# Two decoder layers on one core: the order of three engines between the halves of the layers, written by hand without weight splits

## The chip, the cores and the metric

The kernel runs on one core of a Trainium2 chip. A core has five engines that work beside each other, each taking its own instructions in order and waiting for the others through semaphores: TensorE (PE in the rows, its weight loads PEld), VectorE (DVE), ScalarE (ACT), GpSimd (POOL) and SyncE (SP), which here starts all the transfers. The metric is the device time of one execution in microseconds (us). TensorE's granted clock is at full speed throughout the profiled execution.

## The reference

`x` is 256 rows of 1024 numbers in float32. Layer 0 normalises it, projects it, runs two kinds of attention and an output projection, adds the result to `x`, and then a feed-forward. Layer 1 has a gated spatial mixer and a convolution in place of the attention. Cut to its frame:

```python
for i in range(DEPTH):                     # two layers
    h = rms_norm(x, attn_norm_g[i])
    if i % 2 == 0:
        mix = even_mixer(h, ...)           # differential and block-sparse attention, 8 heads each
    else:
        mix = odd_mixer(h, ...)            # spatial gating, 31-tap causal convolution
    x = x + mix
    x = x + swiglu(rms_norm(x, ffn_norm_g[i]), ffn_w_in[i], ffn_w_out[i])

def rms_norm(x, g):
    return x * rsqrt(mean(x * x, axis=-1) + EPS) * g

def swiglu(h, w_in, w_out):
    g, u = split(h @ w_in, 2)              # 1024 -> 2 x 2816
    return (silu(g) * u) @ w_out
```

## The kernel before, in words

**Precision by splits.** Each float32 operand of a product is kept as two parts: `hi` (rounded by ScalarE while it copies) and `lo` (VectorE subtracts `hi` from the value). A product is three matmuls, hi x hi, hi x lo and lo x hi (`passes`, L225 to L227). Weights come in blocks of 1 MB by SyncE into three buffers `raw`, and each block is split in two halves: `whi` (L131, ScalarE) and `wlo` (L135, VectorE, for some blocks GpSimd). `pump(n)` writes out the next n of these waiting split steps; `ahead` puts a block's four steps in the waiting list; `held` keeps the list from being worked off beside the matmuls.

**The order.** TensorE's order is the program's. The other engines' order is made by a list scheduler, except inside `in_order(...)`, where the named engines keep the order in which the code writes their instructions. Instructions from outside such a region can still be placed between those of the region.

**The boundary, `close`.** It stands three times between a projection and what follows: site 0 between the attention's output projection and the first feed-forward, site 1 between that feed-forward and the odd mixer, site 2 between the odd mixer's output projection and the second feed-forward. The 256 rows are two halves m = 0, 1 of 128, the 1024 columns two halves n. While TensorE still does the last eight steps (`tail_steps`) for m = 1, half m = 0 is closed: VectorE adds the residual into `xs` (L358), ScalarE squares it with a row sum `ss` (L302), VectorE makes `st` (L307, L308), GpSimd raises it to the power -0.5 (`rm`, L310), VectorE multiplies the rows with it (`scr`, L331, one for each n). Then `norm_T` (L340) transposes one column half on TensorE, and `split` copies it to `xT` as hi (ScalarE, L239) and lo (VectorE, L240). Half m = 1 follows the same way inside `follow`, beside the first steps of the next part (`first_steps` of the feed-forward: 16 steps of three matmuls of 256 columns for m = 0, or `gv_steps(0)`: 8 steps of 512 columns). `first_steps` takes columns 0 to 511 in its first four steps and the others after them. `first_T` (L444) transposes the first feed-forward result; it comes six steps into `first_steps` for m = 1 and needs the silu (ScalarE, L436) and a product (VectorE, L437) of the 16 steps for m = 0.

The tables that place these pieces, at the head of the kernel: `SPLITS[site]` how many split steps are written out in the region, `N_T0` and `N_T1` after which step the transposes stand.

**The start and the odd mixer.** `prep` makes the products of a query or key projection that need no scale, and a `scaled` step (L627) for keys; `qk_T` (L638) transposes the result. `PUMPS` says how many split steps stand between. In the odd mixer `spatial` (L1127 to L1135) is TensorE's gating product, ScalarE's scaling L1131, GpSimd's sum and product, ScalarE's hi and GpSimd's lo; L1156 is a one-column silu that loads ScalarE's table ahead of its use.

Of the kernel before, what the change touches and what calls it, by code (L numbers as in the profile page):

```python
# [22 lines left out]
F32 = mybir.dt.float32  # L23
FR = mybir.dt.float32r
AF = mybir.ActivationFunctionType
# [3 lines left out]
P = 128  # L29
S = 256  # L30
# [13 lines left out]
PACE = (3, 1, 2, 1)  # L44

WARM = (5, 4)
PUMPS = (0, 9, 7)

SCALE_FROM, T_FROM = 1, 2
SCALE_AT = 4  # L50
T_AT = 3


LAG = 2
# [1 line left out]
SHARES = (5, 4, 4, 5, 4, 1, 7, 5, 1, 1, 5, 4, 0, 1, 5, 0, 3, 2, 2, 7, 2)  # L56


SPLITS = ((2, 3, 7), (12, 4, 0), (7, 3, 5))
N_T0 = (5, 4, 5)  # L60
N_T1 = (10, 5, 10)


TAP_RATE = 0.55
# [6 lines left out]
def trunk_kernel(ctx: ExitStack, tc: tile.TileContext, a: dict, out: bass.AP):  # L71
    nc = tc.nc
# [5 lines left out]
    small = ctx.enter_context(tc.tile_pool(name="small", bufs=3))  # L78
# [15 lines left out]
    plan, blocks, todo = [], {}, deque()  # L94
# [76 lines left out]
    def pump(n):  # L171
        for _ in range(min(n, len(todo))):
            b, f, step = todo.popleft()
            step(f)
            if step == b.split_lo:
                b.left[f] = 0
                if f == 1:
                    b.load_next()
# [36 lines left out]
    for j in range(2):  # L215
        plan_w(("gu", j), a["odd_w_in"][0], 0, KT, j * 256, 256, "c", lo_engine=nc.gpsimd)
    plan_out("oo", a["odd_w_out"][0], KT, lo_engine=nc.gpsimd)
    for b in (blocks["cg", 0], blocks["ca", 0]):
        b.lo_engine[1] = nc.vector
    blocks["oo", 4].lo_engine = [nc.vector] * 2  # L220
    plan_ffn(1)

# [19 lines left out]
    def in_order(*engines):  # L242

        region = ExitStack()
        region.enter_context(tc.manual_schedule(engines={getattr(mybir.EngineType, e) for e in engines}))
        return region
# [5 lines left out]
    ident = consts.tile([P, P], F32, name="ident")  # L252
# [26 lines left out]
    def col(name, i):  # L279
        return vec[:, rows[name] + i:rows[name] + i + 1]  # L280
# [40 lines left out]
        nc.sync.dma_start(g, bcast(src))  # L321
        return g

    def norm_rows(m, ss, gB, splits):

        r = row_factor(ss)
        pump(splits)
        xn = []
        for n in range(2):
            xn.append(scratch())  # L330
            nc.vector.scalar_tensor_tensor(xn[n], xs[:, m, n * 512:(n + 1) * 512], r, gB[:, n * 512:(n + 1) * 512],  # L331
                                           op0=ALU.mult, op1=ALU.mult)
        return xn

    def norm_T(m, n, xn, xT, ptag):

        pt = ptag()
        ms = slice(m * P, (m + 1) * P)
        for j in range(4):
            nc.tensor.transpose(pt[:, j * P:(j + 1) * P], xn[n][:, j * P:(j + 1) * P], ident)  # L340
        split(xT[0][:, 4 * n:4 * n + 4, ms], xT[1][:, 4 * n:4 * n + 4, ms], pt.rearrange("p (a b) -> p a b", b=P))
# [30 lines left out]
    def close(site, lhs, ws, k0, pss, gB, ptag, tail0=True):  # L372


        xT = new_xT()
        ss = [small.tile([P, 2], F32, name="ss") for _ in range(MT)]

        def end(m, n):
            residual(m, n, pss)
            square(m, n, ss[m])  # L380

        if tail0:
            for n, k in tail_steps(lhs, ws, k0, 0, pss, BY_COLS):
                if (n, k) == (0, 3):
                    end(0, 0)
        else:
            end(0, 0)
        held[0] = True
        region = in_order("DVE", "Pool")
        end(0, 1)  # L390
        xn0 = norm_rows(0, ss[0], gB, SPLITS[site][0])
        for i, (n, k) in enumerate(tail_steps(lhs, ws, k0, 1, pss, BY_BLOCK)):
            if i == 3 and ws[0].index + 4 < len(plan):
                plan[ws[0].index + 4].ahead()
            if i == N_T0[site]:
                norm_T(0, 0, xn0, xT, ptag)
                pump(SPLITS[site][1])
            if k == 3:
                end(1, n)
        norm_T(0, 1, xn0, xT, ptag)  # L400
        xn1 = norm_rows(1, ss[1], gB, SPLITS[site][2])

        def follow(steps, ptag):

            for i, _ in enumerate(steps):
                if 0 <= i - N_T1[site] < 2:
                    norm_T(1, i - N_T1[site], xn1, xT, ptag)
            held[0] = False
            region.close()

        return xT, follow
# [74 lines left out]
    xT = new_xT()  # L486
    rx = []
    with tc.tile_pool(name="attn", bufs=1) as ap, tc.tile_pool(name="pat", bufs=1, space=bass.MemoryType.PSUM) as pat:
# [165 lines left out]
        def prep(name, ps, m, n, want_scaled):  # L654
            t1, scaled = qk_prep(name, ps, m, n, want_scaled)
            pending.append((name, t1, m))
            to_scale.append(scaled)
# [3 lines left out]
        pump(PUMPS[0])  # L661
        prep("dk", ps_dk[0], 0, 32, True)
        pump(PUMPS[1])
        prep("dk", ps_dk[1], 1, 32, True)
        pump(PUMPS[2])
        held[0] = False
        start.close()

# [172 lines left out]
        def projections(jobs):  # L841


            for name in jobs:
                ws = [blocks[name, h] for h in range(2)]
                for m in range(MT):
                    turn = turns[0]
                    turns[0] += 1
                    for k, ps in enumerate(project(ws, m)):
                        if k == SCALE_AT and turn >= SCALE_FROM and to_scale:  # L850
                            to_scale.popleft()()
                        if k == T_AT and turn >= T_FROM and pending:
                            qk_T(*pending.popleft())
                        if ps is None:
                            yield
                    if name in ("dv", "mv"):
                        v_prep(name, ps, m)
                    else:
                        prep(name, ps, m, 32 if name[0] == "d" else 64, name[1] == "k")
                    yield  # L860
# [140 lines left out]
    with tc.tile_pool(name="odd", bufs=1) as op, tc.tile_pool(name="pod", bufs=1, space=bass.MemoryType.PSUM) as pod:  # L1001
# [120 lines left out]
        def spatial(p):  # L1122
            pg = mm_bank() if p % 2 else tq()
            for c in range(MT):
                for h in range(2):
                    g = 2 * p + h
                    nc.tensor.matmul(pg[h * 64:(h + 1) * 64, c * P:(c + 1) * P], gn[:, c, g * 64:(g + 1) * 64],  # L1127
                                     wsT[:, g, :], start=True, stop=True)
            sgt = scratch()[:, :S]
            sgv = sgt.rearrange("p (a b) -> p a b", b=P)  # L1130
            nc.scalar.activation(sgt, pg[:, :S], AF.Copy, scale=col("ln_g", p))  # L1131
            nc.gpsimd.tensor_tensor(sgv, sgv, biasT[:, p, None, :].to_broadcast([P, MT, P]), op=ALU.add)
            nc.gpsimd.tensor_tensor(sgt, sgt, guT[:, p, :], op=ALU.mult)
            nc.scalar.activation(cT[0][:, p, :], sgt, AF.Copy)
            nc.gpsimd.tensor_tensor(cT[1][:, p, :], sgt, cT[0][:, p, :].bitcast(F32), op=ALU.subtract)  # L1135

        pool_order = in_order("Pool")
        gated(0)
# [11 lines left out]
            next(taps)  # L1150
        for m in range(MT):
            gv_norm(m)
        last = project_gu(1)
        with tc.issue_after(last.ins):

            nc.scalar.activation(small.tile([P, 2], F32, name="st2")[:, 0:1], ident[:, 0:1], AF.Silu)  # L1156
        for p in range(4):
            spatial(p)
            for _ in range(2):
                next(taps)  # L1160
        run(taps)
# [167 lines left out]
```

## Time and profile before

| | |
|---|---|
| Median of three runs | 614.56 us (613.72 to 616.35) |
| The profiled execution's own time | 616.31 us |
| Its span, first to last instruction | 614.6 us |
| Busy: TensorE, VectorE, ScalarE, GpSimd | 600.3, 409.7, 345.9, 96.7 us |
| TensorE's weight loads | 512.3 us, beside the matmuls |

Busy time is the time in which an engine has an instruction running. TensorE's matmuls overlap each other in the profile, so its busy time also holds small delays between starts. The profiled execution is 0.3% above the median; differences are worked out in its times and then put onto the median.

### The profile page before, as it was taken

To read this page: it belongs to the slowest core of one execution; us is meant where nothing else is said; L and a number is where in the kernel's file an instruction comes from. 1 tells how busy PE (TensorE), PEld (TensorE's weight loads), DVE (VectorE), ACT (ScalarE), POOL (GpSimd) and SP (SyncE) were. 2 spreads that over 40 slices of the span, in tenths; PEclk is the share of its full clock that TensorE was granted. 3 is DMA by queue.
4 is the path that set the end of the run, shared out by engine and by line. 5 is a ranking of instruction groups with operands and counts; after the bars stand their busy time and mean duration, and the time that the engine had idled before them with its cause. 6 is when DMAs were issued, how large, how long until landed. Compare 5 with 4: busy or idle time off the path is not lost. (4 is left out here: it accounts for less than half of the span.)

```text
span 614.6 us, 8908 instructions
## 1 busy us (share of the span) xinstructions
PE 600.3 (98%) x3420; PEld 512.3 (83%) x3420; DVE 409.7 (67%) x716; ACT 345.9 (56%) x623; POOL 96.7 (16%) x89
## 2 busy tenths in 40 slices
PE   7989999999999999999999999999999999999997
PEld 5867777788888888888886999878988888888886
DVE  3799998648666648664447499877667666664421
ACT  5766768646555596653346955475555556554310
POOL 1951221001000000000004495541000000000000
PEclk9999999999999999999999999999999999999999
DMA  7947216226766527555563463145665556455301
GB/s 243 328 174 272 71 67 206 69 69 207 258 209 185 189 91 274 206 182 176 193 203 102 139 232 130 51 151 182 218 204 185 167 197 206 166 179 204 138 0 69
DMA packets 72791, 104.32 MB, mean 170 GB/s; under 512 B 3068, under 2 KB 56492, under 8 KB 72748
## 3 DMA queue, kind: packets, MB, share of 16 engines
q1 hardware_dynamic: 72748, 103.74, 50.5%
q8 instruction: 27, 0.44, 0.3%
q14 instruction: 16, 0.13, 0.1%
HBM read 102.69 MB, written 1.05 MB: 169 GB/s over the span
## 5 line engine op out<-in xcount | busy, mean ns | idle before, releaser
L131 ACT ACTIVATE whi<-raw 128x1024 fp32r<-128x1024 f32 (+1 forms) x192 | 197.6, 1041 | 175.4 <-PE mm L233 79.4
L135 DVE TENSOR_TENSOR wlo<-raw,whi 128x1024 fp32r<-128x1024 f32 (+1 forms) x174 | 210.1, 1213 | 123.4 <-ACT whi L131 121.8
L233 PE MATMUL mm<-xT,whi 128*128 128x512 f32 x640 | 226.0, 398 | 0.0
L234 PE MATMUL mm<-xT,wlo 128*128 128x256 f32 x640 | 179.6, 281 | 0.0
L233 PEld LDWEIGHTS mm<-xT,whi 128*128 128x128 f32 x640 | 120.1, 188 | 28.9 <-issue 0.2
L234 PEld LDWEIGHTS mm<-xT,wlo 128*128 128x128 f32 x640 | 120.9, 189 | 0.0
L227 PE MATMUL mm<-whi,hT_lo 128*128 128x512 f32 (+1 forms) x176 | 66.5, 378 | 0.0
L226 PE MATMUL mm<-wlo,hT_hi 128*128 128x512 f32 (+1 forms) x176 | 66.5, 378 | 0.0
L225 PE MATMUL mm<-whi,xT 128*128 128x512 f32 (+1 forms) x176 | 66.0, 375 | 0.4 <-ACT xT L545 0.4
L225 PE MATMUL mm<-whi,hT_hi 128*128 128x512 f32 (+1 forms) x176 | 66.4, 377 | 0.0
L227 PE MATMUL mm<-whi,xT 128*128 128x512 f32 (+1 forms) x176 | 63.0, 358 | 1.2 <-DVE xT L240 1.1
L226 PE MATMUL mm<-wlo,xT 128*128 128x512 f32 (+1 forms) x176 | 62.6, 355 | 0.0
L135 POOL TENSOR_TENSOR wlo<-raw,whi 128x1024 fp32r<-128x1024 f32 (+1 forms) x18 | 41.3, 2331 | 21.9 <-ACT whi L131 21.9
L227 PEld LDWEIGHTS mm<-whi,xT 128*128 128x128 f32 x176 | 33.6, 191 | 7.1 <-DVE xT L240 2.0
L225 PEld LDWEIGHTS mm<-whi,xT 128*128 128x128 f32 x176 | 33.6, 191 | 6.9 <-issue 1.3
L225 PEld LDWEIGHTS mm<-whi,hT_hi 128*128 128x128 f32 x176 | 33.1, 188 | 6.4
L226 PEld LDWEIGHTS mm<-wlo,hT_hi 128*128 128x128 f32 x176 | 33.1, 188 | 6.4
L227 PEld LDWEIGHTS mm<-whi,hT_lo 128*128 128x128 f32 x176 | 33.1, 188 | 6.3
L310 POOL TENSOR_TENSOR rm<-st,neg_half 128x1 f32<-128x1 f32 x8 | 8.0, 1002 | 186.1 <-DVE st L308 186.1
L464 DVE TENSOR_TENSOR scr<-mm,scr 128x256 f32<-128x256 f32 x80 | 33.2, 417 | 5.7 <-ACT scr L463 5.7
L226 PEld LDWEIGHTS mm<-wlo,xT 128*128 128x128 f32 x176 | 33.7, 192 | 3.8 <-DVE wlo L135 0.2
L1077 DVE SCALAR_TENSOR_TENSOR cv<-cpad,cw,cv 128x256 f32<-128x256 f32 x87 | 35.8, 479 | 0.3
(226 smaller groups left out, 843.3 us busy)
## 6 DMA issues: line engine op xcount, KB each, us to landing
raw<-in_ffn_w_in SPq DMA_DIRECT2D x44, 1024.0 KB
raw<-in_ffn_w_out SPq DMA_DIRECT2D x22, 1024.0 KB
raw<-in_even_w_in SPq DMA_DIRECT2D x10, 1024.0 KB
raw<-in_odd_w_in SPq DMA_DIRECT2D x8, 1024.0 KB
raw<-in_even_w_out SPq DMA_DIRECT2D x4, 1024.0 KB
raw<-in_odd_w_out SPq DMA_DIRECT2D x4, 1024.0 KB
xs<-in_x SPq DMA_DIRECT2D x4, 256.0 KB
raw<-in_even_w_in SPq DMA_DIRECT2D x4, 256.0 KB
```

What stands on the lines that cost most here:

```text
L131: nc.scalar.activation(self.half(f)[0][:, r], self.source(f)[:, r], AF.Copy)
L135: self.lo_engine[f].tensor_tensor(lo[:, r], self.source(f)[:, r], hi[:, r].bitcast(F32), op=ALU.subtract)
L225: nc.tensor.matmul(ps, lhs[0], rhs[0], start=first, stop=False)
L226: nc.tensor.matmul(ps, lhs[0], rhs[1], start=False, stop=False)
L227: nc.tensor.matmul(ps, lhs[1], rhs[0], start=False, stop=last)
L233: nc.tensor.matmul(bank, w[0], x[2][:, k, :, :].rearrange("p a b -> p (a b)"), start=k == 0, stop=False)
L234: nc.tensor.matmul(bank[:, :S], w[1], x[0][:, k, :], start=False, stop=k == KT - 1)
L310: nc.gpsimd.tensor_tensor(r, t[:, 1:2], neg_half[:, :1], op=ALU.pow)
L464: nc.vector.tensor_tensor(s, bank[:, :S], s, op=ALU.add)
L1077: nc.vector.scalar_tensor_tensor(conv[:, ct, :] if t == TAPS - 1 else acc, cpad[:, ct, t:t + S], cw[:, t, ct:ct + 1], acc, op0=ALU.mult, o ...
```

## The change

At the three sites the region now holds ScalarE's order too, and all waiting split steps are written out ahead of it (`pump(len(todo))`). Inside, `SPLITS` is now two numbers per site, (0, 0), (2, 2) and (0, 0): ahead of and behind the second half's normalisation. The transposes of m = 0 stand behind steps 5 and 6 everywhere; those of m = 1 behind steps 12 and 15 of `first_steps` at sites 0 and 2 (10 and 11 before), and behind 6 and 7 of `gv_steps` at site 1 (5 and 6 before). At the start the scaling of the first `dk` half is written out between the splits, and the transposes of the second one stand behind step 7 of their projection. The silu that loads a table moves behind the second `spatial` scaling. One block's low half goes from GpSimd to VectorE. No arithmetic changes.

```diff
-PUMPS = (0, 9, 7)
-SCALE_FROM, T_FROM = 1, 2
+PUMPS = (0, 5, 4, 7)
+SCALE_FROM, T_FROM = 2, 2
-T_AT = 3
+T_AT = (3, 3, 3, 7, 3, 3, 3, 3, 3, 3, 3, 3)
-SPLITS = ((2, 3, 7), (12, 4, 0), (7, 3, 5))
-N_T0 = (5, 4, 5)
-N_T1 = (10, 5, 10)
+SPLITS = ((0, 0), (2, 2), (0, 0))
+N_T0 = (5, 6)
+N_T1 = ((12, 15), (6, 7), (12, 15))
...
-    for b in (blocks["cg", 0], blocks["ca", 0]):
-        b.lo_engine[1] = nc.vector
+    blocks["cg", 0].lo_engine[1] = nc.vector
+    blocks["ca", 0].lo_engine = [nc.vector] * 2
...
-    def norm_rows(m, ss, gB, splits):
+    def norm_rows(m, ss, gB):
         r = row_factor(ss)
-        pump(splits)
...
         held[0] = True
-        region = in_order("DVE", "Pool")
+        pump(len(todo))
+        region = in_order("DVE", "Pool", "Activation")
         end(0, 1)
-        xn0 = norm_rows(0, ss[0], gB, SPLITS[site][0])
+        xn0 = norm_rows(0, ss[0], gB)
         for i, (n, k) in enumerate(tail_steps(lhs, ws, k0, 1, pss, BY_BLOCK)):
             if i == 3 and ws[0].index + 4 < len(plan):
                 plan[ws[0].index + 4].ahead()
-            if i == N_T0[site]:
-                norm_T(0, 0, xn0, xT, ptag)
-                pump(SPLITS[site][1])
+            if i in N_T0:
+                norm_T(0, N_T0.index(i), xn0, xT, ptag)
             if k == 3:
                 end(1, n)
-        norm_T(0, 1, xn0, xT, ptag)
-        xn1 = norm_rows(1, ss[1], gB, SPLITS[site][2])
+        pump(SPLITS[site][0])
+        xn1 = norm_rows(1, ss[1], gB)
+        pump(SPLITS[site][1])
         def follow(steps, ptag):
             for i, _ in enumerate(steps):
-                if 0 <= i - N_T1[site] < 2:
-                    norm_T(1, i - N_T1[site], xn1, xT, ptag)
+                if i in N_T1[site]:
+                    norm_T(1, N_T1[site].index(i), xn1, xT, ptag)
...
         pump(PUMPS[1])
+        to_scale.popleft()()
+        pump(PUMPS[2])
         prep("dk", ps_dk[1], 1, 32, True)
-        pump(PUMPS[2])
+        pump(PUMPS[3])
...
-        last = project_gu(1)
-        with tc.issue_after(last.ins):
-            nc.scalar.activation(small.tile([P, 2], F32, name="st2")[:, 0:1], ident[:, 0:1], AF.Silu)
+        project_gu(1)
         for p in range(4):
-            spatial(p)
+            last = spatial(p)
+            if p == 1:
+                with tc.issue_after(last.ins):
+                    nc.scalar.activation(small.tile([P, 2], F32, name="st2")[:, 0:1], ident[:, 0:1], AF.Silu)
```

What the built programs hold at three places follows (numbers behind a name tell buffers apart). First VectorE at site 2, from the two multiplies of half m = 0 on, before and then after the change; `xT<-cv2` and `xT<-cv1` are the low parts of the two column halves.

```order
L331 SCALAR_TENSOR_TENSOR scr_4246<-xs_75,rm_4244,gB_4060 128x512
L331 SCALAR_TENSOR_TENSOR scr_4248<-xs_75,rm_4244,gB_4060 128x512
L240 TENSOR_TENSOR xT_4186<-cv2_3308,xT_4186 128x4x128
L135 TENSOR_TENSOR wlo_4275<-raw_4153,whi_4274 128x1024
L358 TENSOR_TENSOR xs_75<-mm_4064,xs_75 128x512
L358 TENSOR_TENSOR xs_75<-mm_4065,xs_75 128x512
L240 TENSOR_TENSOR xT_4186<-cv1_3307,xT_4186 128x4x128
L307 TENSOR_SCALAR st2_4299<-ss_4188 128x1
L308 TENSOR_SCALAR st2_4299<-st2_4299 128x1
L135 TENSOR_TENSOR wlo_4279<-raw_4153,whi_4278 128x1024
```

The same place in the changed kernel:

```order
L330 SCALAR_TENSOR_TENSOR scr_4246<-xs_75,rm_4244,gB_4060 128x512
L330 SCALAR_TENSOR_TENSOR scr_4248<-xs_75,rm_4244,gB_4060 128x512
L135 TENSOR_TENSOR wlo_4384<-raw_4153,whi_4383 128x1024
L135 TENSOR_TENSOR wlo_4394<-raw_4153,whi_4393 128x1024
L240 TENSOR_TENSOR xT_4186<-cv2_3308,xT_4186 128x4x128
L357 TENSOR_TENSOR xs_75<-mm_4064,xs_75 128x512
L135 TENSOR_TENSOR wlo_4406<-raw_4209,whi_4405 128x1024
L135 TENSOR_TENSOR wlo_4421<-raw_4209,whi_4420 128x1024
L240 TENSOR_TENSOR xT_4186<-cv1_3307,xT_4186 128x4x128
L357 TENSOR_TENSOR xs_75<-mm_4065,xs_75 128x512
L307 TENSOR_SCALAR st2_4292<-ss_4188 128x1
L308 TENSOR_SCALAR st2_4292<-st2_4292 128x1
```

The four splits, which come from outside the region, have moved ahead of the two low parts, and none stands behind L308 any more. Site 0 reads alike; ahead of its first multiplies a split has gone from behind L308 too. In both, ScalarE keeps its two pairs of high halves where they were, and its square of the first column half of m = 1 now stands ahead of its copy of T01.

Next GpSimd at site 1, from the power of half m = 0 to the splits behind that of m = 1, before and then after:

```order
L310 TENSOR_TENSOR rm_3228<-st2_3225,neg_half_84 128x1
L135 TENSOR_TENSOR wlo_3257<-raw_3148,whi_3256 128x1024
L135 TENSOR_TENSOR wlo_3261<-raw_3187,whi_3260 128x1024
L1051 MEMSET cpad_3348 128x4x30
L310 TENSOR_TENSOR rm_3289<-st2_3286,neg_half_84 128x1
L135 TENSOR_TENSOR wlo_3400<-raw_3203,whi_3399 128x1024
```

Between the two powers one split is left in the changed kernel:

```order
L310 TENSOR_TENSOR rm_3228<-st2_3225,neg_half_84 128x1
L1053 MEMSET cpad_3348 128x4x30
L135 TENSOR_TENSOR wlo_3279<-raw_3148,whi_3278 128x1024
L310 TENSOR_TENSOR rm_3285<-st2_3282,neg_half_84 128x1
L135 TENSOR_TENSOR wlo_3400<-raw_3203,whi_3399 128x1024
L135 TENSOR_TENSOR wlo_3416<-raw_3373,whi_3415 128x1024
```

It needs the high half `whi_3278`. Where that stands shows ScalarE at the same site, changed kernel, from the last square of m = 0 to the copy of T10 (`xT<-cv2`); `diag2` are diagonal tiles for the convolution.

```order
L302 ACTIVATE scr_3223,ss_3171<-xs_75 128x512
L239 ACTIVATE xT_3170<-tq_3252 128x4x128
L931 ACTIVATE diag2_3501<-ident_78,cw2_1587 128x128
L302 ACTIVATE scr_3260,ss_3172<-xs_75 128x512
L239 ACTIVATE xT_3170<-tq_3265 128x4x128
L931 ACTIVATE diag2_3501<-ident_78,cw2_1587 128x128 x6
L302 ACTIVATE scr_3276,ss_3172<-xs_75 128x512
L131 ACTIVATE whi_3278<-raw_3148 128x1024
L131 ACTIVATE whi_3291<-raw_3187 128x1024
L131 ACTIVATE whi_3363<-raw_3148 128x1024
L131 ACTIVATE whi_3381<-raw_3187 128x1024
L239 ACTIVATE xT_3170<-cv2_3308 128x4x128
```

Before, the two high halves of GpSimd's splits stood between the last square of m = 0 and the copy of T00; now all four stand behind the last square of m = 1.

## Rows read from the trace of the kernel before

**Rows 1.** The page's first part: busy us, share of the span, instructions.
```profile
PE 600.3 (98%) x3420; PEld 512.3 (83%) x3420; DVE 409.7 (67%) x716; ACT 345.9 (56%) x623; POOL 96.7 (16%) x89
```

**Rows 2.** TensorE's waits, whole span: us in total, times, longest us.
```profile
PE tq L638 <- DVE t L627: 1.7, 2, 1.1
PE cv L340 <- DVE scr L331: 1.6, 1, 1.6
...
PE tq L340 <- DVE scr L331: 1.2, 3, 0.6
PE mm L227 <- DVE xT L240: 1.1, 2, 0.6
PE tq L1127 <- ACT scr L1131: 0.7, 1, 0.7
...
PE tq L718 <- DVE e L747: 0.4, 1, 0.4
```

**Rows 3.** Busy us of PE, PEld, DVE, ACT, POOL from 31 to 81.
```profile
31.00:81.00 50.00, 47.90 (x256) 37.17 (x254) 49.57 (x132) 34.69 (x79) 14.88 (x8) 1.00 0.51 179
```

**Rows 4.** TensorE's timeline, site 2: start us, us, what, [idle before <-releaser].
```profile
419.61 0.60 PE L340 MATMUL cv<-ident,scr 128*128 128x128 f32 x4
...
421.44 0.60 PE L340 MATMUL cv<-ident,scr 128*128 128x128 f32 x4
...
423.71 0.28 PE L226 MATMUL mm<-wlo,xT 128*128 128x256 f32 x1
424.54 0.39 PE L227 MATMUL mm<-whi,xT 128*128 128x256 f32 x1 [0.56 <-DVE xT L240]
...
427.62 0.63 PE L340 MATMUL tq<-ident,scr 128*128 128x128 f32 x4 [0.55 <-DVE scr L331]
```

**Rows 5.** VectorE's timeline at the same site.
```profile
418.52 1.42 DVE L331 SCALAR_TENSOR_TENSOR scr<-xs,rm,gB 128x512 f32<-128x512 f32 x2 [0.66 <-POOL rm L310]
420.87 0.69 DVE L240 TENSOR_TENSOR xT<-cv,xT 128x512 fp32r<-128x512 f32 x1 [0.93 <-ACT xT L239]
...
422.61 1.28 DVE L358 TENSOR_TENSOR xs<-mm,xs 128x512 f32<-128x512 f32 x2
423.81 0.68 DVE L240 TENSOR_TENSOR xT<-cv,xT 128x512 fp32r<-128x512 f32 x1
...
425.06 1.22 DVE L135 TENSOR_TENSOR wlo<-raw,whi 128x1024 fp32r<-128x1024 f32 x1
```

**Rows 6.** ScalarE's timeline at the same site.
```profile
417.76 2.01 ACT L131 ACTIVATE whi<-raw 128x1024 fp32r<-128x1024 f32 x2 [0.59 <-PE mm L227]
420.24 0.60 ACT L239 ACTIVATE xT<-cv 128x512 fp32r<-128x512 f32 x1 [0.47 <-PE cv L340]
420.94 2.01 ACT L131 ACTIVATE whi<-raw 128x1024 fp32r<-128x1024 f32 x2
...
423.33 0.63 ACT L302 ACTIVATE scr<-xs 128x512 f32<-128x512 f32 x1
```

**Rows 7.** GpSimd's timeline: a split at site 1, the two powers of site 2.
```profile
344.91 2.41 POOL L135 TENSOR_TENSOR wlo<-raw,whi 128x1024 fp32r<-128x1024 f32 x1 [7.51 <-ACT whi L131]
...
417.94 0.55 POOL L310 TENSOR_TENSOR rm<-st,neg_half 128x1 f32<-128x1 f32 x1 [11.05 <-DVE st L308]
425.22 1.46 POOL L310 TENSOR_TENSOR rm<-st,neg_half 128x1 f32<-128x1 f32 x1 [6.74 <-DVE st L308]
```

**Rows 8.** ScalarE's timeline at site 1: nine diagonal tiles.
```profile
335.49 2.72 ACT L929 ACTIVATE diag<-ident,cw 128x128 fp32r<-128x128 f32 x9
```

**Rows 9.** Timelines of TensorE, ScalarE and VectorE at site 0.
```profile
148.13 0.60 PE L340 MATMUL tq<-ident,scr 128*128 128x128 f32 x4
149.38 1.28 ACT L436 ACT_TABLE_LOAD   x1
151.21 0.41 DVE L437 TENSOR_TENSOR scr<-mm,scr 128x256 f32<-128x256 f32 x1
152.15 0.38 PE L444 MATMUL tq<-ident,scr 128*128 128x128 f32 x2
```

More of the change, by code (lines that the diff above doesn't have):

```diff
@@ L851, in projections @@
                             to_scale.popleft()()
-                        if k == T_AT and turn >= T_FROM and pending:
+                        if k == T_AT[turn] and turn >= T_FROM and pending:
                             qk_T(*pending.popleft())
@@ L1130, in spatial @@
             sgv = sgt.rearrange("p (a b) -> p a b", b=P)
-            nc.scalar.activation(sgt, pg[:, :S], AF.Copy, scale=col("ln_g", p))
+            scaled = nc.scalar.activation(sgt, pg[:, :S], AF.Copy, scale=col("ln_g", p))
             nc.gpsimd.tensor_tensor(sgv, sgv, biasT[:, p, None, :].to_broadcast([P, MT, P]), op=ALU.add)
@@ L1135, in spatial @@
             nc.gpsimd.tensor_tensor(cT[1][:, p, :], sgt, cT[0][:, p, :].bitcast(F32), op=ALU.subtract)
+            return scaled
         pool_order = in_order("Pool")
```

## The prediction

> **What bounds the kernel now.** I read the page first: TensorE works 98% of the span, every other engine far less [rows 1]. So time can only come from the 14 us in which TensorE is idle or restarting, and a change of the other engines' order is worth what it adds to or takes from TensorE's waits. The list of these waits [rows 2] is short: the two transposes of `dk` that wait for VectorE's scaling (L638, 1.7 us), the transposes and low parts at the three boundaries (L340 and L227; 1.6 + 1.2 + 1.1 us), one wait for ScalarE at `spatial` (0.7), one for VectorE's `e` in the attention (0.4). I call the boundaries A (attention to first feed-forward), B (to the odd mixer) and C (to the second feed-forward), and the four groups of transposes of each T00, T01, T10, T11 (row half, column half). After a wait TensorE also restarts about 0.15 us late: at C the matmul at 424.54 had 0.56 us of idle time, but stands 0.83 us behind the one before, where 0.12 is usual [rows 4]. With restarts, and with waits too short for that list, A, B and C cost 1.9, 2.4 and 1.6 us from start to start.
>
> Next I read how the boundary runs at C, engine by engine [rows 4 to 6], because that chain is what the new order rebuilds: VectorE's two normalising multiplies, T00, ScalarE's copy (hi), VectorE's subtraction (lo, 0.69 us), the residual (0.64 us each), ScalarE's square (0.63 us), GpSimd's power, again two multiplies.
>
> **The start.** The change scales the first `dk` half two weight splits earlier and puts the second one's transposes four steps later, so the two waits of 1.7 us [rows 2], 2.0 with restarts, shrink. The first goes. The second scaling comes a split and a little later (1.4 us), its transposes four steps of 0.70 later, but TensorE is 0.8 earlier and waits some 0.5 for the PSUM bank that VectorE frees behind one more split. By this estimate 0.9 is left, and 1.1 gained at that place. But from 31 to 81 us VectorE is busy 49.57 of 50.00 us [rows 3], with the same instructions in both kernels, and at the end of that stretch TensorE waits for VectorE's `e` (L718) [rows 2]. TensorE merely arrives there earlier and waits longer. So I take 0, hidden by VectorE's own work. Bounds: a gain of 1.7 if nothing swallows it, and a loss of 0.5 if ScalarE, which now has a split of late weights ahead of a square, leaves VectorE idle in this full stretch.
>
> **The table load.** It stood ahead of the first `spatial` scaling, 1.28 us long like the one at 149.38 [rows 9], and TensorE waited for that scaling [rows 2]. Behind the second scaling it runs while GpSimd has its two sums to do. Gain: the 0.7 us with its restart, 0.8; nothing if GpSimd's chain to the output projection grew, but that now starts earlier.
>
> **Boundary C.** VectorE's order changes most: two splits stand ahead of the lo of T00 and two ahead of the lo of T01, where there was one in all. They are ready to go, but an engine takes its instructions in order. A split is 1.22 us [rows 5], a pair 2.4.
> - The multiplies end at 419.94 (418.52 + 1.42). Pair: 422.3. Lo of T00: 422.95 instead of 421.56. TensorE, whose T01 now stands one step earlier, starts the first layer's steps at 421.8 and wants this lo as its third matmul, at 422.0: it waits 0.9.
> - Residual 423.6. ScalarE, now bound to the written order, does the square (0.63) before the copy of T01 (0.60), behind two splits that end at 422.95 [rows 6]: hi of T01 at 424.8. TensorE wants it in the fifth step, at 424.2: 0.6.
> - Second pair 425.9, lo of T01 426.6. Wanted at 425.05: 1.5.
> - Residual, square, the two small factors, power (0.55), multiply: 429.75. TensorE, at 0.37 us a step (ten steps and a transposition from 148.13 to 152.15 [rows 9]), reaches T10 after step 12 at 429.6: 0.2.
> Sum 3.2, before 1.6: **C loses 1.6 to 1.8**, I take 1.7.
>
> **Power.** GpSimd's power takes 0.55 us where VectorE does nothing (417.94, between its row factors and its multiplies at 418.52), and 1.46 us with a split running beside it (425.22, split at 425.06) [rows 5, 7]. The new order keeps VectorE empty there at A and in all three T10 chains, so I use 0.55; at 1.46 in these four places the sum would be 3.6 us longer. The Trainium skill (SBUF — State Buffer, Who interferes with whom) says why: a VectorE instruction with two SBUF inputs locks out a GpSimd instruction that reads SBUF until it is done. The trace agrees, 1.46 against 0.55 us.
>
> **Boundary A.** The same chain with the same pairs. The power ahead of T00 shrinks by 0.9 us, so the first wait is 0.4 instead of 0.9; then 0.55, 1.45, 0.3: 2.7. But T11 moves from step 11 to step 15, and what follows it here is ScalarE's table load. Before, T11 at 148.13 led through the load (149.38, 1.28 us) and the silu to VectorE's product, done at 151.62, 3.5 us behind; TensorE's next transposes (L444) came at 152.15 without a wait. Now only six steps lie between: 0.36 + 6 x 0.36 = 2.5 us behind T11. They wait 1.05. Sum 3.75, before 1.9: **A loses 1.9**. At C no table load follows, and the product is there in time.
>
> From the load's end (150.66) to the product's start (151.21) are 0.55 us, which the silu and its handing over fill. On the load the Trainium skill (ScalarE: Activation LUTs, What ACT_TABLE_LOAD costs) states 1283 ns and then 1380 ns of drain for each switch. The trace agrees with the first and shows no drain; with one A would lose 1.4 more.
>
> **Boundary B.** Here GpSimd's queue decides. Before, it took two weight splits early, 327 to 334 us; now one of them stands between the square of the second row half and its power, and its high half is the ScalarE instruction after that square. I count from T00's start: copy done at 1.3; lo 1.95; residual 2.6; square 3.3; copy of T01 3.85; six diagonals of 0.30 us (2.72 for nine [rows 8]) 5.6; square 6.3; high half 7.3; GpSimd's low half, 2.41 us [rows 7], 9.8; power 10.35; multiply 11.1. TensorE has T00, T01, two steps and then seven, 0.70 us each (419.61 to 421.44 holds one T and two [rows 4]): 7.1. T10 waits 4.0. Then VectorE does a split (1.22) before the lo of T10 and another before that of T11, and the projection, which needs both row halves at once, waits 0.7 and 0.3. Sum 5.0, before 2.4: **B loses 2.6**. GpSimd's split no longer meets VectorE's multiplies, which frees T01, and this is in the sum.
>
> **Loads.** SP gets one weight load ahead of `gB` at A and two behind it at C; none of TensorE's waits [rows 2] names a weight transfer, so nothing, and under 1 us if one came late.
>
> **Sum.** 1.9 + 2.6 + 1.7 - 0.8 + 0 = 5.4 us. Made against the profiled execution (616.31, span 614.60) it is 621.7; that execution is the slow end of the three, so from the median 614.56 I predict 620.0.
>
> **Rivals.**
> - The start's gain comes through: VectorE's full stretch has slack that the busy share hides. 620.0 - 1.1 = 618.9. For it: TensorE's wait for `e` is only 0.4 us. Against: 49.57 of 50 us. Chance 0.12.
> - Not slower: the pairs hold up nothing at A and C. It decides itself at one point: VectorE must have both splits behind it when the copy of T00 (and of T01) is done, at C 420.84, which needs their start 1.5 us before the multiplies end. Then A and C lose only the 1.05 us behind the table load: 620.0 - 2.7 - 3.2 = 614.1. For it: their high halves are done at 419.77, about then. Against: the written order has the multiplies first. Chance 0.10.
> - B is cheaper: GpSimd's split finds its high half early and only the old wait remains, 620.0 - 2.6 = 617.4. Against: the square is ahead of the high half in ScalarE's order. Chance 0.08.
> - The power stays at 1.46 although VectorE is empty: 0.9 each at A's first and at the three T10 chains, 623.6. Chance 0.05.
> - ScalarE stays shut behind the table load longer than the row of it leaves room for [rows 9], so that L444 waits longer at A: 0.5 us of it make 620.5. Chance 0.03. By the Trainium skill's drain (the page named at A) this case would be 621.4.
> - As forecast: 0.62, with its own range of 618.3 to 621.7 (0.8 us either way at each boundary, adding as independent errors, and 0.5 at the start).
>
> **How the numbers follow.** 0.5% of 614.56 is 3.1 us, about what a measurement of this kernel can tell from no change. Slower (over 617.6): nearly all of the forecast, the start's, the power's and the drain's cases and half of B's, less some for what I cannot see: 0.77. Same: the rest of B's and the pairs' case, 0.15. Faster: the pairs free and the start's gain together, 0.08. The range leaves out the pairs' case below and the power's above, and takes in B's: 616.5 to 622.5.
>
> **What would show it.** Right: at C two splits ahead of the first lo, and TensorE waiting three times for xT in the first-layer steps; at A a wait at L444 for VectorE; at B one wait of about 4 us at T10, with GpSimd's split ending just ahead of the power; powers of 0.55; no wait at `spatial`; the waits at L638 smaller and that for `e` longer by as much. Wrong: lo of T00 done within 0.8 us of its hi, a T10 wait at B under 2 us, or TensorE ahead of the old kernel by 1 us at 100 us.

## The result: slower by 1.1%, and the profile after

The changed kernel takes 622.19 us (median of six runs, 620.03 to 625.07) against 614.83 us; the ratio is 1.0112, 95% interval 1.0093 to 1.0132. Forecast were 620.0 us and a range of 616.5 to 622.5. The profiled execution takes 622.48 us, 6.2 more than that of before, whose second feed-forward ran 1.9 us slower at the same granted clock (last section); without that difference the change costs 8.1. The page's first part and its line of granted clock, in 40 equal slices of the span:

```profile
PE 603.6 (97%) x3420; PEld 516.4 (83%) x3420; DVE 408.8 (66%) x717; ACT 347.9 (56%) x623; POOL 90.4 (15%) x88
...
PEclk9999979998999999999999899999999999999999
```

The work is that of [rows 1]. New is the clock: three slices stand below full speed, where the kernel before had none. TensorE's waits (us in total, times, longest) answer to [rows 2]:

```profile
PE cv L339 <- DVE scr L330: 4.0, 1, 4.0
PE mm L227 <- DVE xT L240: 3.1, 4, 1.1
...
PE mm L225 <- ACT xT L239: 0.8, 2, 0.4
PE po L730 <- ACT wT L722: 0.7, 1, 0.7
PE tq L444 <- DVE scr L437: 0.7, 1, 0.7
PE tq L720 <- DVE e L749: 0.4, 1, 0.4
```

One wait of 4.0 us is T10 at B, the four of 3.1 are the low parts at A and C, L444 waits behind the table load. The wait at `spatial` and both at L638 are gone; in the attention stands a new one (L730) ahead of that for `e`. L331 to L358 are now L330 to L357, and the attention's lines are two higher.

At C, VectorE's timeline [rows 5] now reads:

```profile
425.11 1.41 DVE L330 SCALAR_TENSOR_TENSOR scr<-xs,rm,gB 128x512 f32<-128x512 f32 x2 [0.66 <-POOL rm L310]
426.44 2.35 DVE L135 TENSOR_TENSOR wlo<-raw,whi 128x1024 fp32r<-128x1024 f32 x2
428.71 0.68 DVE L240 TENSOR_TENSOR xT<-cv,xT 128x512 fp32r<-128x512 f32 x1
...
429.91 2.35 DVE L135 TENSOR_TENSOR wlo<-raw,whi 128x1024 fp32r<-128x1024 f32 x2
432.18 0.68 DVE L240 TENSOR_TENSOR xT<-cv,xT 128x512 fp32r<-128x512 f32 x1
```

and TensorE's [rows 4], the four places where it waits:

```profile
429.45 0.39 PE L227 MATMUL mm<-whi,xT 128*128 128x256 f32 x1 [0.59 <-DVE xT L240]
...
431.28 0.39 PE L225 MATMUL mm<-whi,xT 128*128 128x256 f32 x1 [0.39 <-ACT xT L239]
...
432.91 0.39 PE L227 MATMUL mm<-whi,xT 128*128 128x256 f32 x1 [1.12 <-DVE xT L240]
...
436.27 0.63 PE L339 MATMUL tq<-ident,scr 128*128 128x128 f32 x4
```

Each low part ends right behind a pair of splits (428.71 + 0.68, 432.18 + 0.68), and the matmul that reads it starts 0.05 to 0.06 us later. From start to start these places cost 0.75, 0.55, 1.28 and 0.27 us.

At B, in one timeline of ScalarE and GpSimd [rows 7], the late chain is complete: square, four high halves, GpSimd's split, its power.

```profile
339.00 0.62 ACT L302 ACTIVATE scr<-xs 128x512 f32<-128x512 f32 x1
...
339.61 3.89 ACT L131 ACTIVATE whi<-raw 128x1024 fp32r<-128x1024 f32 x4
...
340.74 2.35 POOL L135 TENSOR_TENSOR wlo<-raw,whi 128x1024 fp32r<-128x1024 f32 x1 [4.63 <-ACT whi L131]
...
343.05 0.55 POOL L310 TENSOR_TENSOR rm<-st,neg_half 128x1 f32<-128x1 f32 x1
```

At A, timeline of ScalarE, VectorE and TensorE [rows 9]: the table load now ends 0.9 us before L444.

```profile
153.94 1.28 ACT L436 ACT_TABLE_LOAD   x1
...
155.23 0.39 ACT L436 ACTIVATE scr<-mm 128x256 f32<-128x256 f32 x1
...
155.65 0.42 DVE L437 TENSOR_TENSOR scr<-mm,scr 128x256 f32<-128x256 f32 x1 [1.00 <-ACT scr L436]
...
156.13 0.44 PE L444 MATMUL tq<-ident,scr 128*128 128x128 f32 x2 [0.69 <-DVE scr L437]
```

What no step of the forecast has shows the view of stretches (busy us and instructions of PE, PEld, DVE, ACT, POOL; then granted clock, DMA share, GB/s):

```profile
79.60:86.40 6.80, 6.80 (x21) 4.62 (x21) 6.79 (x24) 3.83 (x12) 1.96 (x2) 0.50 0.00 0
86.40:100.00 13.60, 13.60 (x87) 11.38 (x86) 11.00 (x30) 9.13 (x21) 1.31 (x1) 1.00 0.45 143
...
147.90:151.20 3.30, 3.30 (x18) 3.30 (x17) 1.78 (x4) 0.00 (x0) 0.56 (x1) 0.50 0.89 292
...
345.90:349.20 3.30, 3.29 (x16) 2.99 (x15) 3.30 (x6) 2.80 (x10) 0.00 (x0) 0.50 0.48 161
```

At 0.50, that is at 1.2 GHz in place of 2.4, a 512-column matmul starts every 0.43 us instead of 0.23, a 256-column one every 0.21 instead of 0.12. For the first stretch the same instructions can be timed in both kernels, from the first transposition of `e` to the matmul behind L638. Before:

```profile
80.43 0.83 PE L718 MATMUL tq<-ident,e 128*128 128x128 f32 x4 [0.36 <-DVE e L747]
...
84.79 0.48 PE L225 MATMUL mm<-whi,xT 128*128 128x512 f32 x1
```

After:

```profile
79.26 1.08 PE L720 MATMUL tq<-ident,e 128*128 128x128 f32 x4 [0.40 <-DVE e L749]
...
86.71 0.47 PE L225 MATMUL mm<-whi,xT 128*128 128x512 f32 x1
```

They take 7.45 us in place of 4.36, so 3.1 us. In the other two stretches, each matmul against the usual step of its shape, it is 1.5 and 1.3 us. Each stretch stands right behind waits: those of L730 and L720 (78.21 and 79.26), those of A (143 to 147), that of T10 (340.5 to 344.5).

So the question for the experiments: how much of the loss is waits, how much is the clock that follows them, and which edit makes the waits?

### The profile page after: what moved, and what is told of

It reads as the page before. It is cut to its first block, busy times and chain, and to the rows that moved or that the text cites. A ratio compares the mean times of both kernels' runs of the same rounds, so it can differ in the third digit from the quotient of the medians.

```text
span 620.6 us, 8910 instructions
## 1 busy us (share of the span) xinstructions
PE 603.6 (97%) x3420; PEld 516.4 (83%) x3420; DVE 408.8 (66%) x717; ACT 347.9 (56%) x623; POOL 90.4 (15%) x88
## 3 DMA queue, kind: packets, MB, share of 16 engines
HBM read 102.69 MB, written 1.05 MB: 167 GB/s over the span
## 5 line engine op out<-in xcount | busy, mean ns | idle before, releaser
L225 PE MATMUL mm<-whi,xT 128*128 128x512 f32 (+1 forms) x176 | 67.0, 381 | 0.8 <-ACT xT L239 0.8
L227 PE MATMUL mm<-whi,xT 128*128 128x512 f32 (+1 forms) x176 | 64.1, 364 | 3.1 <-DVE xT L240 3.1
L135 POOL TENSOR_TENSOR wlo<-raw,whi 128x1024 fp32r<-128x1024 f32 (+1 forms) x17 | 38.4, 2285 | 25.6 <-ACT whi L131 25.6
L227 PEld LDWEIGHTS mm<-whi,xT 128*128 128x128 f32 x176 | 34.4, 195 | 8.8 <-DVE xT L240 3.9
L225 PEld LDWEIGHTS mm<-whi,xT 128*128 128x128 f32 x176 | 34.4, 195 | 8.3 <-issue 1.7
L310 POOL TENSOR_TENSOR rm<-st,neg_half 128x1 f32<-128x1 f32 x8 | 4.4, 552 | 191.4 <-DVE st L308 191.4
```

Of the source, the lines that this page charges most:

```text
L135: self.lo_engine[f].tensor_tensor(lo[:, r], self.source(f)[:, r], hi[:, r].bitcast(F32), op=ALU.subtract)
L225: nc.tensor.matmul(ps, lhs[0], rhs[0], start=first, stop=False)
L227: nc.tensor.matmul(ps, lhs[1], rhs[0], start=False, stop=last)
L310: nc.gpsimd.tensor_tensor(r, t[:, 1:2], neg_half[:, :1], op=ALU.pow)
```

## The experiments

The kernel before ran beside every group. "Mean clock" is the mean granted clock over the span, averaged over the timed executions; the kernel before had 0.9987 to 0.9996 in the groups.

| Run | Ratio to before | Mean clock |
|---|---|---|
| new start and table load, old boundaries | 0.9992 (0.9972 to 1.0012) | 0.997 |
| changed, old start | 1.0078 (1.0051 to 1.0106) | 0.995 |
| changed, filled wait at B | 1.0111 (1.0069 to 1.0152) | 0.994 |
| changed, GpSimd's split late | 1.0132 (1.0097 to 1.0167) | 0.989 |
| changed, again | 1.0122 (1.0101 to 1.0143) | 0.989 |
| changed, waits filled, fill at A late | 1.0175 (1.0153 to 1.0197) | 0.991 |
| changed, old split places at A and C | 1.0170 (1.0150 to 1.0190) | 0.988 |
| first run, filled | 1.0011 (0.9993 to 1.0028) | 0.998 |
| changed, old site 1 | 1.0061 (1.0041 to 1.0082) | 0.995 |
| changed, old site 1, filled | 1.0024 (1.0006 to 1.0042) | 0.999 |
| changed, ScalarE free | 0.9984 (0.9968 to 1.0000) | 0.996 |
| changed, ScalarE free, filled | 0.9997 (0.9979 to 1.0014) | 0.998 |

**Only what lies outside the boundaries.** The kernel before with

```diff
-PUMPS = (0, 9, 7)
-SCALE_FROM, T_FROM = 1, 2
+PUMPS = (0, 5, 4, 7)
+SCALE_FROM, T_FROM = 2, 2
```

and the rest of the change's start and table load.

> The kernel before with the change's start and table load, and the old boundaries. The prediction's theory (the start's gain ends in VectorE's full stretch, the table load gives 0.8): 614.0 us, wait for e longer by about 2. Rival one (the start's gain of 1.9 comes through and nothing takes it): 612.1. Rival two, from the trace of the changed kernel: the start gives 1.9 by 77 us, then TensorE's clock falls to half for 5 to 6 us and takes 3 back, table load 0.8: 615.3, with granted clock near 0.5 between 81 and 86 us.

The same time as before: 0.9992 of 614.83 is 614.3, and the interval reaches from 613.1 to 615.6. So rival one (612.1) falls, and the time cannot tell the theory (614.0) from rival two (615.3). TensorE's wait at `spatial` is gone here and in every run with the moved load. The start is settled by one distance that does not depend on when the first weights arrive: from VectorE's first key product (L621) to its `e`. Before:

```profile
28.30 0.74 DVE L621 SCALAR_TENSOR_TENSOR t<-mm,rm,gC_dk 128x512 f32<-128x512 f32 x1
...
79.90 0.47 DVE L747 SCALAR_TENSOR_TENSOR e<-e,dc 128x256 f32<-128x256 f32 x1
```

After:

```profile
27.77 0.74 DVE L621 SCALAR_TENSOR_TENSOR t<-mm,rm,gC_dk 128x512 f32<-128x512 f32 x1
...
78.72 0.48 DVE L749 SCALAR_TENSOR_TENSOR e<-e,dc 128x256 f32<-128x256 f32 x1
```

51.60 us against 50.95, and 50.98 in this run: of the 0.65 us, 0.43 are VectorE's last idle time in this stretch [rows 3], which closes (0.01 is left in the changed kernel), and little else can be had. TensorE's lead at L638 (2.0 us with restarts) ends in longer waits at 78 and 79 us, as the forecast had it, but 0.6 us come through, not 0. The half clock did not come in this profiled execution, although it makes both waits; of its twelve timed executions four have a mean clock of 0.994 and four of 0.999 or more, so it comes in some and not in others.

**The changed kernel with the old start**, the same lines the other way round.

> The changed kernel with the old start; boundaries and table load as changed. The prediction's theory (the start is worth 0): 622.2 us, as the changed kernel. Rival one (the start's gain of 1.9 came through): 624.1. Rival two (the start nets a loss of 1.2 by the half clock behind 80 us, which needs the new start): 621.0, no stretch at half clock before 139 us; those at the first two boundaries stay.

VectorE's distance is 51.62 us again. No stretch at half clock lies ahead of 340 us. The median, 622.24 us beside 616.97, is 0.3% nearer to the kernel before than the changed kernel's, which speaks for rival two, though the changed kernel's was measured in another group and the intervals overlap.

**A filled wait at B.** In `norm_T`, for T10 at site 1 alone:

```diff
         pt = ptag()
+        for _ in range(fill):      # 30
+            nc.tensor.transpose(pt[:, :P], ident, ident)
```

> The changed kernel with 30 transposes of the identity, some 3.3 us of TensorE's time, written out ahead of the transposes T10 at site 1, where TensorE waits 4.1 us. Theory (the wait itself brings the clock down): granted clock 1.0 from 345 to 352 us, and 1.2 us gained, 621.0. Rival (the low clock has another cause and comes anyway): 0.5 for some 3 us behind T10 and 622.2.

The profiled execution has clock 1.00 from 340 to 350 us, as the theory has it. But the scheduler, which prices the fill, put a third split ahead of the low part of T10, and the projection waits 3.0 us for it, from start to start, at 347.6. Behind that unfilled wait the clock stays at 1.00 too, so this run is weak support for the theory, and it gives no verdict on the time.

**GpSimd's split behind the power.** `SPLITS[1]` is (0, 4).

> The changed kernel with all four of site 1's split steps behind the second normalisation (SPLITS (0, 4) in place of (2, 2)), so that no split stands ahead of GpSimd's second power. The prediction's theory (GpSimd's queue decides the wait at T10): the power starts some 2.8 us sooner, the wait at T10 falls from 4.1 to 1.3, the low parts behind it wait 1.2 more, 620.6 us, or 619.4 if the low clock behind T10 goes with it. Rival (the diagonals and the square ahead decide): the wait stays near 4 and the time at 622.2.

Half a miss. The power comes at once, at 339.29, and so do the multiplies:

```profile
339.29 0.56 POOL L310 TENSOR_TENSOR rm<-st,neg_half 128x1 f32<-128x1 f32 x1 [4.16 <-DVE st L308]
339.81 2.35 POOL L135 TENSOR_TENSOR wlo<-raw,whi 128x1024 fp32r<-128x1024 f32 x1
339.88 3.49 DVE L330 SCALAR_TENSOR_TENSOR scr<-xs,rm,gB 128x512 f32<-128x512 f32 x2 [0.74 <-POOL rm L310]
```

GpSimd's queue did hold T10 back. But now the same split runs beside VectorE's multiplies, which take 3.49 us in place of 1.42 (the first alone 2.83), and T10 still waits 3.3 us. The split costs 2.4 us ahead of the power and 2.1 behind it.

**The changed kernel again**, without an edit.

> The changed kernel itself once more, beside the others on one chip. If TensorE's low clock comes by chance behind waits: ratio to the kernel before near 1.011, mean granted clock from 0.985 to 0.997 in most executions, another one in each, and the time following it. If the low clock belonged to that one profiled execution: mean clock 1.0 in most, and 1.004, which is the waits alone (2.6 us).

All five executions have a mean clock of 0.986 to 0.994; the profiled one is at half clock behind the same three places and behind C.

**Fills in the waits at 78 and 79 us, at A and at B.** The transposes at A went into a bank of their own, declared with the pool of the feed-forward.

> The changed kernel with transposes of the identity in TensorE's waits: 10 in the two at 78 and 79 us, 18 in the three of boundary A, 7 ahead of L444, 16 (1.7 of 4.1 us) ahead of T10 at B. They end before the wait would, so that they take no time by themselves. Theory (waits bring the low clock, and it costs some 4 to 5 us): mean granted clock 0.998 or more in most executions, 617.5 us or a ratio of 1.004. Rival (the low clock has another cause): clock near 0.990 and 1.011 as without them.

Neither came. That bank was one that T01 still held, so the fill itself waited:

```profile
PE junk L342 <- DVE xT L246: 3.8, 1, 3.8
```

With this longer wait at A the half clock followed there; it also came behind the 2.1 us left at B, and at C, where nothing was filled. Only the place at 78 us is a clean trial: no wait, no half clock.

**Old split places at A and C.**

```diff
-SPLITS = ((0, 0), (2, 2), (0, 0))
+SPLITS = ((2, 3, 7), (0, 0, 2, 2), (7, 3, 5))
```

with `pump` at its old places in the region (`pump(len(todo))` at site 1 only), ScalarE still bound.

> The changed kernel with the weight splits of sites 0 and 2 placed as before (2, 3, 7 and 7, 3, 5 inside the region), ScalarE still in the written order and the transposes at the new steps. The prediction's theory (the pairs of splits ahead of the low parts make the waits at A and C): the low part of T00 is done 2.3 us sooner behind the multiplies, the three waits for xT shrink to one of 0.7, 1.3 us gained at each site, ratio 1.007, or 1.004 if A's low clock goes too; L444 still waits 0.85. Rival (ScalarE's order or the later transposes make them): the waits and 1.011 stay.

The low part of T00 is in time now and its wait is gone; so the pair did make it. But the time is worse. ScalarE at A:

```profile
140.25 0.60 ACT L239 ACTIVATE xT<-tq 128x512 fp32r<-128x512 f32 x1 [2.67 <-PE tq L340]
140.75 3.89 ACT L131 ACTIVATE whi<-raw 128x1024 fp32r<-128x1024 f32 x4
144.53 0.62 ACT L302 ACTIVATE scr<-xs 128x512 f32<-128x512 f32 x1
...
145.15 0.58 ACT L239 ACTIVATE xT<-tq 128x512 fp32r<-128x512 f32 x1
```

Bound to the written order, ScalarE does four high halves and the square ahead of the copy of T01, and TensorE waits for that copy, 2.3 us at each of A and C. Here a split written into the region held up one engine or the other.

**The first run, filled**: ten transposes at 78 and 79 us and twelve at T10 of B.

> The kernel before with the change's start and table load and the old boundaries (as in the first run), and transposes of the identity in TensorE's waits at 78 and 79 us (10) and ahead of T10 at B (12). Theory (the start's 1.1 and the table load's 0.8 are real, and the low clock took them back): mean clock 0.999 or more, 613.0 us, ratio 0.997. Rival (nothing to be had there): ratio 1.000 and a mean clock as in the first run (0.997).

The clock came as the theory says (ten of twelve executions at 0.999 or more; four of twelve without the fills), the gain did not. In the profiled execution TensorE waits 0.57 and 0.69 us, from start to start, at two places where the first run's does not, one in the attention and one in the odd mixer, where the scheduler's order has changed; and it is at half clock for 10 us behind 98 us. What the start and the table load are worth, some 1.4 us by the trace, was too little for this measurement.

**Site 1 as before, without and with fills.** A pair that differs in nothing but the fills and one high half in the attention (the traces show the other engines' instructions in the same order): in both, site 1 has its old region, splits and steps, and one block's low half is back on GpSimd. The fill at A and C goes into a bank that the residual has read.

```diff
+FILL_STEPS = ((3, 4, 11), (3, 4, 11))   # ahead of the late lo, hi and lo of T00 and T01
+FILL_FIRST = (7, 0)                     # ahead of L444
+FILL_E = (6, 4)                         # at 78 and 79 us
```

> The changed kernel with site 1 as before (order, splits and transposes). Theory (waits, and behind them low clock): against the kernel before, the waits are A +1.3, C +1.2, start about -0.7, table load -0.8, together +1.0; the low clock behind 79 us, A and C costs some 3 us more: 619 us, ratio 1.006, mean clock near 0.992. Rival (the clock belongs to site 1's long wait alone): clock 0.998 or more and 1.002.

> The kernel of the run beside it (site 1 as before) with transposes of the identity in TensorE's waits at 78 and 79 us (10), at A and C (18 each) and ahead of L444 (7), into banks that are free there. All other engines' orders are the same but for one high half in the attention. Theory (TensorE's waits bring the low clock): mean clock 0.998 or more, the same ends of the waits, ratio 1.002. Rival (the low clock does not depend on the waits): clock and ratio as in the run beside it.

Both as the theory has it; the rival that ties the clock to site 1's long wait falls, since the first has half clock without it. Stretches of the first (busy us of the five engines as above; the granted clock is the third figure from the end):

```profile
79.60:86.30 6.70, 6.53 (x20) 4.59 (x21) 6.70 (x23) 4.31 (x14) 1.64 (x1) 0.50 0.00 0
147.80:151.20 3.40, 3.40 (x19) 3.40 (x18) 1.78 (x4) 0.34 (x2) 0.56 (x1) 0.50 0.95 312
431.10:434.50 3.40, 3.40 (x18) 3.40 (x17) 1.78 (x4) 0.72 (x2) 0.55 (x1) 0.50 0.92 305
```

and of the filled one (PE, clock, DMA share, GB/s):

```profile
76.00:90.00 14.00, 13.94 (x90) 1.00 0.21 75
138.00:160.00 22.00, 21.94 (x163) 1.00 0.46 141
420.00:440.00 20.00, 19.62 (x148) 1.00 0.48 159
```

Mean clock 0.995 against 0.999, ratio 1.0061 against 1.0024. The two intervals just touch; the means of the 11 and 12 executions, on one chip, are 2.4 us apart, give or take 1.6. The fills do no useful work, so the clock is what is left to account for what they take off, 2.3 us by the ratios. Within the first of the pair the same shows: its five executions with a mean clock of 0.992 or less take 621.2 to 623.0 us, its three at 1.000 618.5 to 619.0, and its three at 0.997 anything from 617.0 to 621.6.

**ScalarE free.**

```diff
-        region = in_order("DVE", "Pool", "Activation")
+        region = in_order("DVE", "Pool")
```

> The changed kernel with ScalarE left out of the written order of the three regions (one word). The scheduler then puts T01's copy ahead of the square, one split instead of two ahead of the low part of T00, and site 1's high halves ahead of the squares of the second row half. Theory (ScalarE's binding is what makes the pairs and GpSimd's late split): the waits at A, B and C fall to about those of before (1.9, 2.4, 1.6), ratio 1.003. Rival (the emptied split places in VectorE's order make them): waits as in the changed kernel, 1.011.

This one word takes the whole loss away: 0.9984, against 1.0112 and 1.0122 with it. TensorE's waits:

```profile
PE tq L339 <- DVE scr L330: 3.2, 3, 1.1
...
PE mm L226 <- DVE xT L240: 1.1, 1, 1.1
...
PE mm L227 <- DVE xT L240: 1.1, 3, 0.6
```

From start to start A, B and C cost 2.2, 2.6 and 2.0 us, against 1.9, 2.4 and 1.6 before. The expectation's detail was off: the pair still stands ahead of the low part of T00 at C (0.75 us from start to start, as with ScalarE bound), but none stands ahead of T01's, because ScalarE may now copy T01 ahead of the square:

```profile
423.81 0.58 ACT L239 ACTIVATE xT<-cv 128x512 fp32r<-128x512 f32 x1
424.29 1.05 ACT L131 ACTIVATE whi<-raw 128x1024 fp32r<-128x1024 f32 x1
425.35 0.63 ACT L302 ACTIVATE scr<-xs 128x512 f32<-128x512 f32 x1
```

At B GpSimd's split is done at 333.6 us, long before the power at 338.28; it ran beside the first half's two multiplies, which took 3.60 us, and T01 waited 1.0. Counted from 31 us on, this profiled execution is 1.6 us behind that of the kernel before when the second feed-forward begins, and gets 1.9 back there by the pace of the last section. So by the rows the edit brings the time back to about that of the kernel before, and not below it.

**ScalarE free, filled** at 78 and 79 us.

> The changed kernel with ScalarE left out of the written order, as in the last run, and ten transposes of the identity in TensorE's two waits at 78 and 79 us. Theory (with the waits of the boundaries back at the old size, only the low clock behind 79 us is left to cost something, about 2.5 us): mean clock 0.999 or more, ratio 0.995, faster than both kernels. Rival (VectorE bounds that stretch at either clock): clock 0.999, but the ratio stays at 0.998.

The clock is up (ten of twelve executions at 0.999 or more, against two of twelve), the time is not down: 0.9997, an interval that overlaps the last run's. That the half clock costs nothing there, as the rival has it, does not hold either: in the last run the six executions at 0.997 or more take 613.8 to 614.9 us, the six at 0.994 615.6 to 618.2. (The first run shows no such step: its four at 0.999 or more take 615.8 to 616.7, its four at 0.994 615.6 to 618.8.) The trace shows a part of what takes the fills' gain back: with the clock up TensorE waits 0.6 us for T_mq at 97 us, as it does in the kernel before, and 0.4 for ScalarE's `wT` at 99, and the last run has neither. The rest was not found, and the two runs are from different chips. No version here beats the kernel before by more than the measurement tells.

## Why the prediction was right in its total, and where it was not

**The total was right, its make-up was not.** Forecast were 5.4 us of waits. The traces show 2.9 us of waits (A and C 1.2 each, B 1.9, start -0.6, table load -0.8) and, in the profiled execution, 5.9 us of half clock. Of that 0.7 replaces a wait that the slower TensorE no longer makes:

```profile
PE tq L700 <- ACT T_mq L639: 0.6, 1, 0.6
```

Together 8.1 us, which is what the two profiled executions show (6.2, and the 1.9 of the second feed-forward); by the medians it is 7.4, by the ratio 6.9. That the total came to lie inside the range is luck: the waits are 2.5 us short of the forecast, and a cost that no step had makes up for them and more. The range for "as forecast" was also put a little wide: 0.8 three times and 0.5 add, as independent errors, to 1.5, not 1.7.

**The step that was missing** is the clock. The prediction took every wait at its length. Of the 14 profiled executions, including those of before and after, half clock came at:

| Place | with the new waits | with old or filled waits |
|---|---|---|
| behind 78 to 79 us | 6 of 8 | 0 of 6 |
| A | 6 of 8 | 0 of 6 |
| B (T10 waits over 2 us) | 5 of 6 | 0 of 8 |
| C | 4 of 8 | 0 of 6 |

Beside these one filled execution had it at 98 us, behind two waits there, and none had it anywhere else between the first 14 us and TensorE's end. The kernel before is not free of it: of its 80 executions beside the groups, 12 have a mean clock of 0.996 or 0.997. No trace of one of them was kept, so whether its shorter waits bring it there stays open. That the new waits bring it is shown by the pair with and without fills; why one execution has it at C and another not, these runs do not tell. The Trainium skill (TensorE: Matmul & The Clock Gate, HAM oscillation — how this bites in real kernels) states, of a loop whose bursts of matmuls wait for a transfer, that the wait brings the clock down, so that the next burst starts slow. This case's traces agree as to the order, with waits for other engines in place of transfers: the clock is 1.00 up to 79.6, 147.9 and 345.8 us and 0.50 behind, where the last waits ended at 79.26, 146.58 and 344.53.

**Boundary C** (forecast 1.7 lost): 1.2. The four waits were given as 0.9, 0.6, 1.5 and 0.2, and are 0.75, 0.55, 1.28 and 0.27. **Boundary A** (1.9): 1.2, by 0.40, 0.54, 1.28, 0 and 0.85 against 0.4, 0.55, 1.45, 0.3 and 1.05 (the 0 for T10 is in the half-clock stretch, where TensorE comes there later); L444 does wait for the product behind the table load. The rival of a longer shut ScalarE fell: the silu starts 0.01 us after the load's end. The drain that the Trainium skill states (ScalarE: Activation LUTs, What ACT_TABLE_LOAD costs) shows in no run here: the four loads in mid-kernel are each followed within 0.02 us in all 14 traces.

**Boundary B** (2.6): 1.9. T10's wait was given as 4.0 and is 4.0, by the chain that was named. The two waits behind it were given as 0.7 and 0.3 and are 0.4 and 0.2. The rest is in what was subtracted: with the short losses at T00 and behind a wait counted too, B cost the kernel before 2.7 us from start to start, not 2.4.

**The power** is 0.55 us at all eight places, as said. **The table load** gives 0.8, as said. **The start** was put at 0 and is 0.6; the statement that VectorE swallows the lead holds for the rest of it.

**The reason was half named.** The pairs were taken for the cause at A and C. They are the thing that TensorE waits behind, but the second of them stands ahead of the low part because ScalarE is bound: with ScalarE free it is gone, while the first pair and its wait stay (0.59 us in the list at C with ScalarE bound, 0.60 with it free). Freeing it undoes the loss with the pumps, the steps and VectorE's order rule unchanged. The prediction used the binding only for a square ahead of a copy.

**The rivals.** 0.6 of the start's 1.1 came through. The pairs held up both low parts, so "not slower" fell; GpSimd's split waited for its high half, so "B is cheaper" fell.

## What to carry to other kernels

Price a wait of TensorE at more than its length: here waits of 0.2 to 4.0 us were followed, in most executions, by several microseconds at 1.2 GHz, and in the profiled one that was more than half of the loss. Binding one more engine to a written order moves the instructions from outside the region too: count what then stands ahead of each copy and each low part, on both engines. A waiting split on GpSimd had no free place here: ahead of the power it delays it, behind the power, or beside the multiplies of the first half, it slows VectorE's multiplies (3.49 and 3.60 us in place of 1.42).

## What the runs showed of the hardware

- A VectorE multiply of 128x512 with two SBUF inputs took 2.83 us beside a GpSimd split, 0.75 elsewhere.
- With transposes of the identity in the waits at 78 and 79 us, at A and at C, the granted clock stayed at 1.00 there in the profiled execution.
- With the same program text and granted clock 1.00, TensorE's pace in the second feed-forward differs between the profiled executions by 2%. From 480 to 540 us (PE busy and instructions), first before, then after:

```profile
480.00:540.00 60.00, 60.00 (x342) 1.00 0.57 193
```

```profile
480.00:540.00 60.00, 60.00 (x349) 1.00 0.58 193
```

Over that stage it is 1.9 us, which would account for the 1.5 to 1.8 us by which the profiled execution of before stood above its median. Four of the 14 have the slower pace (341 or 342 instructions), ten the faster (347 to 349). With one trace to a run these runs do not tell whether the execution, the chip or the kernel sets it; if it is the kernel, up to 0.3% of a ratio to the kernel before has nothing to do with waits or clock.
